# Differential attention's keys and queries: rounded on all 128 rows at once, then placed by transfers within SBUF

## The chip, the cores and the metric

The kernel runs on one core of a Trainium2 chip. The metric is the device time of one execution in microseconds (us), median of three runs. TensorE (PE) multiplies matrices, VectorE (DVE) and ScalarE (ACT) do elementwise work and empty PSUM, GpSimd (POOL) does small work, SyncE (SP) issues most of the transfers.

## What is computed

The reference is a two-layer transformer over 256 latent and 256 context tokens of width 1024. Each layer has a feed-forward part, a token mixer (retention in 4 heads beside differential attention in 8 heads) and a second feed-forward part. The change is in the differential attention, whose core is:

```python
q_d = rope_2d(to_diff_heads(dq), row, col)
k_d = rope_2d(to_diff_heads(dk), row, col)
k_all = jnp.concatenate([k_dc, k_d], axis=3)      # context keys are not rotated
s = jnp.einsum('bhiqd,bhikd->bhiqk', q, k) * (DIFF_DH ** -0.5)   # DIFF_DH = 64, two maps
p = jax.nn.softmax(s, axis=-1)
a = p[:, :, 0] - lam * p[:, :, 1]
o = jnp.einsum('bhqk,bhke->bhqe', a, v)
```

Each head has two maps of 64 channels. The rotation turns pairs of channels by an angle that depends on the token's row and column on the grid.

## The kernel before

Weights come from HBM in tiles of 128 x 1024 float32 (`load`, L143, four buffers `raw`, issued on SP). `split` (L151) makes of each a rounded part (ACT, L154) and the rest (DVE, L155) in a tile `w` (five buffers), and every product of a projection is made of three matmuls (`mm3`, L329 to L332): high x high, high x low, low x high. Activations `h` are kept in the same two parts.

The mixer (L451) walks through blocks of the input projection. `projT` (L521) computes a block with channels on the partitions (48 matmuls, of 512 columns for both token groups or 256 for the latents alone), into a pair of PSUM banks or one bank of the ring `main4`; `tok` (L497) computes a block with tokens on the partitions (24 matmuls into one bank). When a block is done, an eviction function empties the bank, and the bank goes back to the ring; the next block that gets it must wait for the eviction's last read.

`diff_blocks(u)` (L871) makes a unit: two heads, one K block (latent and context), then one Q block (both groups in layer 0, the latents in layer 1). There are four units in each of the two layers, and after each of them come token blocks (`rv_block` or `wide`). Its eviction is `ev_diff` (L564). For the latent columns it first calls `rotate` (L545): the block times the cosines (L547), products of row groups with the sines of the partner rows (L550, four groups of 32 rows for this table, two of 64 for the retention's), and a sum (L552). Then, for each of the two maps, it works on the 64 rows that belong to the map. For K, `KH[m]` must hold the rounded key in both halves of the 128 rows, `KL[m]` the rest in both halves: three copies on ACT (L575, L577, L578) and one subtraction on DVE (L576). For Q, `Q[m]` holds the rounded query in the map's own rows (ACT, L571) and the rest in the other rows (DVE, L572), so that one matmul with `KH[m]` (L660) and one with `KL[m]` (L661) give a map's score.

The scores, their softmax, the transposes and the products with V (`diff_attn`, L643) are side work: a generator in a queue, from which `tick` (L476) takes steps at given points of the projections, as many as are due; its argument is how much the point counts. `need` (L489) takes steps until a piece of side work is done. A planner in the framework then orders each engine's instructions and sets the waits on semaphores: the order on an engine is fixed before the run, but it is not simply the order of the source. SP works its queue in order, too: an issue that waits holds up the issues behind it.

`main4` is the ring of PSUM banks that projections use, `side4` that of the side work; `slot` gives one of 20 SBUF tiles of 4 KB per row (`r` in the trace), `tmp4` one of three of the same size (`t4`), which the scores' exponentials use, and `tmp2` one of five of 2 KB (`t2`).

Of the kernel before, what the change touches and what calls it, by code (L numbers as in the profile page):

```python
# [11 lines left out]
F32 = mybir.dt.float32  # L12
F32R = mybir.dt.float32r
BF16 = mybir.dt.bfloat16
AF = mybir.ActivationFunctionType
ALU = mybir.AluOpType
# [18 lines left out]
def build(ctx, tc, a):  # L35
# [415 lines left out]
    def mixer(l, st, AB, fetch, after):  # L451
# [69 lines left out]
        def projT(b, pairs, ev, w):  # L521
            ws = [split(r) for r in load(a["winT"][l, b])]
            n = 256 * len(pairs)
            if len(pairs) == 2:
                b0 = main4.two()
                bk = b0
            else:
                b0 = main4.one()
                bk = b0.rearrange("p (j n) -> p j n", j=2)
            for j in range(2):  # L530
                js = slice(j * P, (j + 1) * P)
                for k in range(KD):
                    wt = ws[k // 4].rearrange("p s (k n) -> p s k n", k=4)
                    mm3(bk[:, j], wt[:, 0, k % 4, js], wt[:, 1, k % 4, js], h[k // 2][:, k % 2, 0, 0:n],
                        h[k // 2][:, k % 2, 1, 0:n], k == 0, k == KD - 1)
                    if k == 7 and j == 0:
                        flush()
                    if j * KD + k in ((3, 7, 11) if len(pairs) == 2 else (7,)):
                        tick(w)
            for c in pairs:  # L540
                ev(c, bk[:, :, c * 256:(c + 1) * 256])
            main4.put(b0)
            tick(w)

        def rotate(b, tab, half):  # L545
            q, w = tmp2([P, 2, 256]), tmp2([P, 2, 256])
            dve.tensor_tensor(out=q, in0=b, in1=tab[:, 0].unsqueeze(1).broadcast_to([P, 2, 256]), op=ALU.mult)  # L547
            for p0 in range(0, P, half):
                p1 = p0 ^ half
                dve.tensor_tensor(out=w[p0:p0 + half], in0=b[p1:p1 + half],  # L550
                                  in1=tab[p0:p0 + half, 1].unsqueeze(1).broadcast_to([half, 2, 256]), op=ALU.mult)
            dve.tensor_tensor(out=q, in0=q, in1=w, op=ALU.add)  # L552
            return q
# [7 lines left out]
                                         op0=ALU.mult, op1=ALU.subtract)  # L561
            return ev

        def ev_diff(H, Lo):  # L564
            def ev(c, b):
                q = rotate(b, dtab, 32) if c == LAT else b
                sl = slice(c * 256, (c + 1) * 256)
                for m in range(2):
                    own, oth = slice(64 * m, 64 * m + 64), slice(64 - 64 * m, 128 - 64 * m)
                    if Lo is None:  # L570
                        act(H[m][own, :, sl], q[own], AF.Copy, scale=0.125)  # L571
                        dve.scalar_tensor_tensor(out=H[m][oth, :, sl], in0=q[own], scalar=0.125,  # L572
                                                 in1=H[m][own, :, sl], op0=ALU.mult, op1=ALU.subtract)
                    else:
                        nc.scalar.copy(H[m][own, :, sl], q[own])  # L575
                        dve.tensor_tensor(out=Lo[m][own, :, sl], in0=q[own], in1=H[m][own, :, sl], op=ALU.subtract)  # L576
                        nc.scalar.copy(H[m][oth, :, sl], q[own])  # L577
                        nc.scalar.copy(Lo[m][oth, :, sl], Lo[m][own, :, sl])  # L578
            return ev

        def ev_V(dst):
# [289 lines left out]
        def diff_blocks(u, before=None):  # L871
            KH = [slot([P, 2, 512], F32R) for _ in range(2)]
            KL = [slot([P, 2, 512], F32R) for _ in range(2)]
            projT(8 + u, BOTH, ev_diff(KH, KL), 0.3)
            if before:
                before()
            Q = [slot([P, 2, 512], F32R) for _ in range(2)]
            projT(4 + u, QP, ev_diff(Q, None), 0.3)
            return KH, KL, Q

        def diff_defer(u, kq, dv, within):
# [224 lines left out]
def rope_tables():  # L1106
    def ang(pos, half):
        inv = (np.float32(10000.0) ** (-np.arange(half, dtype=np.float32) / np.float32(half))).astype(np.float32)
        return (pos.astype(np.float32)[:, None] * inv[None, :]).astype(np.float32)

    t = np.arange(T)
    r = ang(t, 64)
    c, s = np.cos(r), np.sin(r)
    rt = np.stack([np.concatenate([c, c], 1), np.concatenate([-s, s], 1)], 0)
    d = np.concatenate([ang(t // 64, 16), ang(t % 64, 16)], 1)
    c, s = np.cos(d), np.sin(d)
    dt = np.stack([np.concatenate([c, c, c, c], 1), np.concatenate([-s, s, -s, s], 1)], 0)

    def lay(z):
        return np.ascontiguousarray(z.transpose(2, 0, 1), dtype=np.float32)  # L1120
    return lay(rt), lay(dt)
# [6 lines left out]
def layout(i):  # L1128
    f = {k: np.asarray(v) for k, v in i.items()}
    a = {}  # L1130
    a["xin"] = np.concatenate([f["x"][0], f["ctx"][0]], 0).reshape(4, P, D)
    a["ccc"] = np.stack([f["c"][0], f["c_ctx"]], 1).reshape(KD, P, 2).transpose(1, 0, 2)
    a["sel"] = (np.arange(P)[:, None] % 32 == np.arange(2)[None, :]).astype(np.float32)
    a["wada0"] = f["w_ada"][0, :, 0:2 * D].reshape(KD, P, 2, 4, 256).transpose(3, 1, 0, 2, 4).reshape(4, P, 4096)
    a["cc"] = np.stack([f["c"][0], f["c_ctx"]], 0)
    a["wada"] = f["w_ada"].transpose(0, 2, 1).reshape(L, 36, 2, P, D).transpose(0, 1, 3, 2, 4).reshape(L, 36, P, 2 * D)
    a["bada"] = f["b_ada"].reshape(L, 9, 8, P).transpose(3, 0, 1, 2)
    a["nwc"] = f["norm_w"].reshape(L, 6, 8, P).transpose(3, 0, 1, 2)
    a["fin"] = (f["ffn_w_in"].reshape(L, 2, KD, P, 2, NF, P).transpose(0, 1, 5, 3, 2, 4, 6)
                .reshape(L, 2, NF, P, 2048))  # L1140
    a["fout"] = f["ffn_w_out"].reshape(L, 2, NF // 2, 2, P, D).transpose(0, 1, 2, 4, 3, 5).reshape(L, 2, NF // 2, P, 2048)
    cols = np.arange(8192)
    cols[3072:5120] = cols[3072:5120].reshape(32, 2, 2, 16).transpose(0, 2, 1, 3).reshape(-1)
    wi = f["w_in"][:, :, cols].reshape(L, KD, P, 32, 256)
    a["winT"] = wi[:, :, :, TB].transpose(0, 3, 2, 1, 4).reshape(L, 12, P, 2048)
    a["winW"] = wi[:, :, :, WB].reshape(L, KD, P, 10, 512).transpose(0, 3, 2, 1, 4).reshape(L, 10, P, 4096)
    a["wout"] = f["w_out"].reshape(L, 4, 2, P, D).transpose(0, 1, 3, 2, 4).reshape(L, 4, P, 2048)
    a["gnw"] = f["ret_gn_w"]
    a["subw"] = f["diff_subln_w"]
    a["lamv"] = f["diff_lambda"]  # L1150
    a["decay"] = f["ret_decay_logit"].reshape(L, 8)
    a["rtab"], a["dtab"] = rope_tables()
    a["strip"] = strip_table()
    return {k: np.ascontiguousarray(v) for k, v in a.items()}
# [16 lines left out]
```

## Time and profile before

| | us |
|---|---|
| three runs, median | 2194.53 (2194.24 to 2195.38) |
| the profiled execution | 2194.1 |
| its span, first to last instruction | 2192.3 |
| PE busy | 2140.4 (98%) |
| DVE busy | 1365.7 (62%) |
| ACT busy | 865.8 (39%) |
| mean granted clock of TensorE | 0.996 |

Between the span and the execution lie 1.8 us. Busy time of PE counts a matmul to its modelled end, so that neighbours overlap: matmuls of 512 columns are 0.39 us long and start 0.227 us apart. The mixer of layer 0 lies between about 400 and 860 us of the span, that of layer 1 between about 1635 and 1990.

### The profile page before, as it was taken

How to read it: one execution, taken by the hardware profiler on the slowest of the kernel's cores; microseconds unless marked ns; L12 is line 12 of the kernel's file. 1: busy time of each engine (PE TensorE's matmuls, PEld its weight loads, DVE VectorE, ACT ScalarE, POOL GpSimd, SP SyncE). 2: the span in 40 equal slices, each digit the busy share in tenths (PEclk: the TensorE clock that was granted, in tenths of full speed). 3: DMA queues.
4: the chain of work that ended last, by engine and by line, in shares of the span. 5: the costliest groups of instructions: out<-in, count | busy, mean ns of one | idle time of the engine just before them, and what ended most of it. 6: DMA issues, size and time to landing. Idle time of an engine off the chain costs nothing. (4 is left out here: it accounts for less than half of the span.)

```text
span 2192.3 us, 27590 instructions
## 1 busy us (share of the span) xinstructions
PE 2140.4 (98%) x10730; PEld 1790.6 (82%) x10730; DVE 1365.7 (62%) x2108; ACT 865.8 (39%) x1367; POOL 129.1 (6%) x236
## 2 busy tenths in 40 slices
PE   7999999999999999999999999999999999998998
PEld 5888888778788878888888888888878888878997
DVE  4799372678665774596243279825347776787554
ACT  3322332553533553522232242223245544565453
POOL 1000000201010000200000010000010000001000
PEclk9999999999999999999999999999999999999999
DMA  8866342222122234364334247734323323355554
GB/s 332 284 218 217 106 135 96 88 68 85 51 91 98 68 97 148 132 211 155 97 124 139 91 161 224 269 96 134 97 67 109 115 93 108 123 194 174 187 183 134
DMA packets 85060, 306.99 MB, mean 140 GB/s; under 512 B 9968, under 2 KB 10048, under 8 KB 84928
## 3 DMA queue, kind: packets, MB, share of 16 engines
q1 hardware_dynamic: 81936, 296.78, 41.2%
q0 software_dynamic: 2848, 8.43, 1.4%
q8 instruction: 84, 1.38, 0.3%
q14 instruction: 48, 0.39, 0.1%
q10 hardware_dynamic: 144, 0.01, 0.0%
HBM read 304.10 MB, written 1.09 MB: 139 GB/s over the span
## 5 line engine op out<-in xcount | busy, mean ns | idle before, releaser
L155 DVE TENSOR_TENSOR w<-raw,w 128x1024 fp32r<-128x1024 f32 x408 | 497.2, 1222 | 465.6 <-ACT w L154 461.9
L154 ACT CAST w<-raw 128x1024 fp32r<-128x1024 f32 x408 | 427.5, 1053 | 665.4 <-PE ps L332 609.3
L330 PE MATMUL ps<-h,w 128*128 128x512 f32 (+1 forms) x1868 | 664.7, 357 | 4.7 <-ACT w L154 2.6
L331 PE MATMUL ps<-h,w 128*128 128x512 f32 (+1 forms) x1868 | 664.9, 356 | 0.4 <-DVE h L293 0.3
L332 PE MATMUL ps<-h,w 128*128 128x512 f32 (+1 forms) x1868 | 663.6, 356 | 1.2 <-DVE w L155 1.2
L330 PEld LDWEIGHTS ps<-h,w 128*128 128x128 f32 x1868 | 353.4, 190 | 57.2 <-DVE h L292 4.7
L332 PEld LDWEIGHTS ps<-h,w 128*128 128x128 f32 x1868 | 353.8, 190 | 50.6 <-DVE w L155 1.8
L331 PEld LDWEIGHTS ps<-h,w 128*128 128x128 f32 x1868 | 354.1, 190 | 50.2 <-DVE h L293 1.4
L174 DVE CUSTOM_DVE_ANT_0 jd<-r,r 128x1024 bf16<-128x1024 f32 x224 | 273.4, 1221 | 6.8 <-DMA r<-wada_dram 2.0
L330 PE MATMUL ps<-w,h 128*128 128x512 f32 x544 | 216.1, 398 | 15.5 <-ACT r L577 11.9
L331 PE MATMUL ps<-w,h 128*128 128x512 f32 x544 | 214.3, 394 | 0.0
L332 PE MATMUL ps<-w,h 128*128 128x512 f32 x544 | 213.8, 394 | 0.0
L330 PE MATMUL ps<-w,gs 128*128 128x512 f32 x504 | 196.2, 389 | 0.0
L331 PE MATMUL ps<-w,gs 128*128 128x512 f32 x504 | 196.1, 389 | 0.0
L332 PE MATMUL ps<-w,gs 128*128 128x512 f32 x504 | 196.1, 389 | 0.0
L366 ACT ACTIVATE t<-ps 128x512 f32<-128x512 f32 (+1 forms) x88 | 47.9, 545 | 252.0 <-PE ps L332 250.6
L330 PEld LDWEIGHTS ps<-w,h 128*128 128x128 f32 x544 | 102.7, 189 | 38.2 <-ACT r L577 15.2
L367 DVE TENSOR_TENSOR r<-ps,t 128x512 f32<-128x512 f32 (+1 forms) x88 | 54.8, 622 | 105.3 <-PE ps L332 77.7
L331 PEld LDWEIGHTS ps<-w,h 128*128 128x128 f32 x544 | 102.8, 189 | 20.2 <-DVE w L155 1.5
L332 PEld LDWEIGHTS ps<-w,h 128*128 128x128 f32 x544 | 102.5, 188 | 20.4
L330 PEld LDWEIGHTS ps<-w,gs 128*128 128x128 f32 x504 | 94.6, 188 | 19.8
L332 PEld LDWEIGHTS ps<-w,gs 128*128 128x128 f32 x504 | 94.6, 188 | 19.6
(180 smaller groups left out, 2132.8 us busy)
## 6 DMA issues: line engine op xcount, KB each, us to landing
raw<-fin_dram SPq DMA_DIRECT2D x176, 512.0 KB, 4.3
r<-wada_dram SPq DMA_DIRECT2D x144, 512.0 KB, 5.1
raw<-fout_dram SPq DMA_DIRECT2D x88, 512.0 KB, 3.6
raw<-winW_dram SPq DMA_DIRECT2D x80, 512.0 KB, 3.6
raw<-winT_dram SPq DMA_DIRECT2D x48, 512.0 KB, 3.6
raw<-wout_dram SPq DMA_DIRECT2D x16, 512.0 KB, 5.6
r<-scr POOLq DMA_DIRECT2D x10, 512.0 KB, 5.4
r<-cc_dram SPq DMA_DIRECT2D x7, 512.0 KB, 5.2
```

The costliest lines, as they stand in the source:

```text
L154: keep(nc.scalar.copy(w[:, 0, :], src))
L155: keep(dve.tensor_tensor(out=w[:, 1, :], in0=src, in1=w[:, 0, :], op=ALU.subtract))
L174: dve.tensor_tensor_reduce(out=junk, in0=r[j], in1=cs[c], scale=1.0, scalar=0.0, op0=ALU.mult, op1=ALU.add, accum_out=out[:, c, 2 * u + j: ...
L330: mm(o, lhsT=wH, rhs=xH, start=start, stop=False)
L331: mm(o, lhsT=wH, rhs=xL, start=False, stop=False)
L332: mm(o, lhsT=wL, rhs=xH, start=False, stop=stop)
L366: act(sg[:, :N], ab[0][:, :N], AF.Silu)
L367: dve.tensor_tensor(out=g[f // 2][:, f % 2, :N], in0=ab[1][:, :N], in1=sg[:, :N], op=ALU.mult)
```

## The change

The four parts belong together.

1. `ev_diff` becomes `ev_full`, which is like the eviction of the retention's projections: one copy or scaling on ACT for all 128 rows and one subtraction on DVE.
2. The halves that the maps' tiles need are made by transfers: `move` copies two groups of 32 rows (rows 32m to 32m+31 and 64+32m to 64+32m+31) from one SBUF tile to the same or the other groups of another, in two DMAs on SP. A unit has 12 of these for K and 8 for Q. Q's parts are first put into two `t4` tiles. The third move of each K tile writes rows that the first two have read.
3. The columns of the input projection are put in another order (on the host), so that the two halves of a rotation lie 64 rows apart, and the signs in the sine table follow. `rotate` then runs two products of 64 rows instead of four of 32.
4. `projT` evicts the context columns before the latent ones (for the retention's projections, too), and the differential projections count 0.5 per tick point instead of 0.3.

```diff
-            for c in pairs:
+            for c in reversed(pairs):
                 ev(c, bk[:, :, c * 256:(c + 1) * 256])
...
-        def ev_diff(H, Lo):
+        def rows_of(m):
+            return [slice(32 * m + 64 * x, 32 * m + 64 * x + 32) for x in range(2)]
+
+        def move(dst, md, src, ms, n):
+            for rd, rs in zip(rows_of(md), rows_of(ms)):
+                nc.sync.dma_start(dst[rd, :, 0:n].bitcast(F32), src[rs, :, 0:n].bitcast(F32))
+
+        def ev_full(H, Lo, scale):
             def ev(c, b):
-                q = rotate(b, dtab, 32) if c == LAT else b
+                q = rotate(b, dtab, 64) if c == LAT else b
                 sl = slice(c * 256, (c + 1) * 256)
-                for m in range(2):
-                    own, oth = slice(64 * m, 64 * m + 64), slice(64 - 64 * m, 128 - 64 * m)
-                    if Lo is None:
-                        act(H[m][own, :, sl], q[own], AF.Copy, scale=0.125)
-                        dve.scalar_tensor_tensor(out=H[m][oth, :, sl], in0=q[own], scalar=0.125,
-                                                 in1=H[m][own, :, sl], op0=ALU.mult, op1=ALU.subtract)
-                    else:
-                        nc.scalar.copy(H[m][own, :, sl], q[own])
-                        dve.tensor_tensor(out=Lo[m][own, :, sl], in0=q[own], in1=H[m][own, :, sl], op=ALU.subtract)
-                        nc.scalar.copy(H[m][oth, :, sl], q[own])
-                        nc.scalar.copy(Lo[m][oth, :, sl], Lo[m][own, :, sl])
+                act(H[:, :, sl], q, AF.Copy, scale=scale)
+                dve.scalar_tensor_tensor(out=Lo[:, :, sl], in0=q, scalar=scale, in1=H[:, :, sl],
+                                         op0=ALU.mult, op1=ALU.subtract)
             return ev
...
-            projT(8 + u, BOTH, ev_diff(KH, KL), 0.3)
+            projT(8 + u, BOTH, ev_full(KH[0], KL[0], 1.0), 0.5)
+            for K2 in (KH, KL):
+                move(K2[1], 1, K2[0], 1, 512)
+                move(K2[1], 0, K2[0], 1, 512)
+                move(K2[0], 1, K2[0], 0, 512)
             if before:
                 before()
             Q = [slot([P, 2, 512], F32R) for _ in range(2)]
-            projT(4 + u, QP, ev_diff(Q, None), 0.3)
+            qH, qL = tmp4([P, 2, 512], F32R), tmp4([P, 2, 512], F32R)
+            projT(4 + u, QP, ev_full(qH, qL, 0.125), 0.5)
+            for m in range(2):
+                move(Q[m], m, qH, m, 256 * NQ)
+                move(Q[m], 1 - m, qL, m, 256 * NQ)
             return KH, KL, Q
...
-    dt = np.stack([np.concatenate([c, c, c, c], 1), np.concatenate([-s, s, -s, s], 1)], 0)
+    dt = np.stack([np.concatenate([c, c, c, c], 1), np.concatenate([-s, -s, s, s], 1)], 0)
...
-    cols[3072:5120] = cols[3072:5120].reshape(32, 2, 2, 16).transpose(0, 2, 1, 3).reshape(-1)
+    cols[3072:5120] = cols[3072:5120].reshape(16, 2, 2, 2, 16).transpose(0, 3, 1, 2, 4).reshape(-1)
```

## Rows read from the trace of the kernel before

**Rows 1.** The page, first part: busy us (share of the span) x instructions.
```profile
PE 2140.4 (98%) x10730; PEld 1790.6 (82%) x10730; DVE 1365.7 (62%) x2108; ACT 865.8 (39%) x1367; POOL 129.1 (6%) x236
```
**Rows 2.** Waits of PE, 390 to 870: total us, times, longest us.
```profile
PE ps L330 <- ACT r L577: 6.6, 4, 1.7
...
PE ps L660 <- DVE r L572: 0.3, 1, 0.3
```
**Rows 3.** Waits of PE, 1630 to 2000.
```profile
PE ps L330 <- ACT r L577: 5.3, 4, 1.4
PE ps L330 <- DVE t L550: 3.2, 1, 3.2
```
**Rows 4.** Timeline of PE, unit 0, layer 0: start, us, instruction [idle before <-releaser].
```profile
446.43 0.39 PE L331 MATMUL ps<-h,w 128*128 128x512 f32 x1
446.65 0.39 PE L332 MATMUL ps<-h,w 128*128 128x512 f32 x1
448.70 0.50 PE L330 MATMUL ps<-w,h 128*128 128x512 f32 x1 [1.66 <-ACT r L577]
```
**Rows 5.** Timeline of ACT in the same place: K's eviction.
```profile
442.24 0.62 ACT L577 CAST r<-t 64x512 fp32r<-64x512 f32 x1
...
448.07 0.58 ACT L577 CAST r<-ps 64x512 fp32r<-64x512 f32 x1
```
**Rows 6.** Timeline of DVE in the same place.
```profile
436.20 0.69 DVE L547 TENSOR_TENSOR t<-ps,dtab 128x512 f32<-128x512 f32 x1 [0.41 <-PE ps L332]
436.90 2.79 DVE L550 TENSOR_TENSOR t<-ps,dtab 32x512 f32<-32x512 f32 x4
439.72 1.22 DVE L155 TENSOR_TENSOR w<-raw,w 128x1024 fp32r<-128x1024 f32 x1
...
442.24 0.68 DVE L576 TENSOR_TENSOR r<-t,r 64x512 fp32r<-64x512 f32 x1
```
**Rows 7.** DVE's groups by line and shape, whole span: xcount | busy us, mean ns.
```profile
L550 DVE TENSOR_TENSOR t<-ps,rtab 64x512 f32<-64x512 f32 x16 | 11.0, 688 | 0.2
```
**Rows 8.** Timeline of PE, last unit of layer 1.
```profile
1919.07 0.39 PE L330 MATMUL ps<-w,h 128*128 128x512 f32 x1
1922.67 0.47 PE L330 MATMUL ps<-w,h 128*128 128x512 f32 x1 [3.21 <-DVE t L550]
1924.09 0.50 PE L330 MATMUL ps<-w,h 128*128 128x512 f32 x1 [0.95 <-ACT r L577]
```
**Rows 9.** Two stretches: length, busy us of PE, PEld, DVE, ACT, POOL, PEclk, DMA share, GB/s.
```profile
446.00:450.00 4.00, 2.34 (x11) 1.62 (x10) 2.47 (x3) 3.92 (x6) 0.00 (x0) 1.00 0.00 0
1923.00:1929.00 6.00, 5.05 (x15) 3.87 (x15) 5.82 (x7) 3.72 (x6) 0.00 (x0) 0.72 0.28 87
```
**Rows 10.** The page, DMA issues: xcount, KB each, median us from issue to landing.
```profile
raw<-winT_dram SPq DMA_DIRECT2D x48, 512.0 KB, 3.6
...
gnb<-gnw_dram POOLq DMA_DIRECT2D x8, 128.0 KB, 3.2
out_dram<-X SPq DMA_DIRECT2D x4, 256.0 KB, 2.1
```
**Rows 11.** Timeline of SP and ACT after unit 0; SP's issues of `raw` (ns).
```profile
429.65 20.12 SPq L147 DMA_DIRECT2D raw<-winT_dram  x4
...
479.17 2.18 ACT L154 CAST w<-raw 128x1024 fp32r<-128x1024 f32 x2
...
L147 SPq DMA_DIRECT2D raw<-winT_dram x3: 327/328/328, 435.8 to 449.4; - x3
```
**Rows 12.** Timeline of DVE and PE, first score of unit 0.
```profile
456.27 1.40 DVE L572 SCALAR_TENSOR_TENSOR r<-t,r 64x512 fp32r<-64x512 f32 x2
...
457.01 0.50 PE L660 MATMUL ps<-r,r 128*128 128x512 f32 x1
```
**Rows 13.** SP in the first 30 us: timeline, and its waits in the whole span.
```profile
9.52 10.82 SPq L999 DMA_DIRECT2D r<-wada_dram  x8
...
SPq L999 <- DMA r<-wada_dram: 6.5, 7, 0.9
```

## Prediction: what the change does to the time

> **What bounds the kernel now.** I began with the page's first part: TensorE (PE) is busy 98% of the span, VectorE (DVE) 62%, ScalarE (ACT) 39% [rows 1]. So only what PE loses can be won; less work on DVE or ACT is worth nothing by itself. Next came the waits of PE alone, in the stretches of the two mixers. In layer 0 one wait stands out: the first product of a product series waits four times for line 577, 6.6 us together, and nothing else that the change touches reaches 0.4 us [rows 2]. In layer 1 the same wait takes 5.3 us in four places, and a wait for line 550 takes 3.2 us once [rows 3]. Lines 550 and 577 are both evictions of a differential projection. There are 8 units (four in each of two layers), and each has one such place.
>
> The timeline shows one place. The Q projection's last product starts at 446.65; the next token product starts at 448.70, released by ACT line 577 [rows 4]. Products start 0.22 us apart otherwise, so 1.82 us are lost. The token product needs a PSUM bank of the *K* projection, which had ended before DVE began its rotation at 436.20 [rows 6]. From there to the last read of that bank, at 448.07 + 0.58 = 448.65 [rows 5], go 12.4 us. The reader sees why: DVE takes four 32-row products (2.79 us together) before ACT can start [rows 6], then ACT makes 12 half-width copies of about 0.6 us, with a weight cast between them. Each copy covers 64 partitions but costs what 512 columns cost.
>
> **The change, part by part.** The time of an instruction here goes by its columns: the 32-row products take 0.70 us each [rows 6], the 64-row products of the retention table 0.688 us [rows 7]. So two products of 64 rows replace four of 32 at the same price each, and one full-width copy replaces six half ones.
>
> K's eviction becomes: context first, one ACT copy (0.6) and one DVE subtraction (0.69), then for the latent columns one product, two products and a sum (four of 0.69) and again one copy and one subtraction. The bank's last PSUM read is the second 64-row product: 436.20 + 0.6 + 0.69 + 3 x 0.69 = 439.6, or 440.8 with the weight subtraction of 1.22 us that DVE had in between [rows 6]. PE asks for the bank at 446.65 + 0.23 = 446.9. A margin of 6 us remains, so this wait goes entirely. In layer 1 the Q product series has half as many columns, but there PE passes through one whole token tile before it asks.
>
> What goes: layer 0, 4 x 1.82 = 7.3 us. Layer 1, first three places: idle 5.3 - 0.95 = 4.35 [rows 3, 8], plus 0.17 each, since idle counts from a product's end (0.39 long) and not from the next start at 0.22: 4.85 us. The last place is the worst: starts at 1919.07, 1922.67 and 1924.09 [rows 8] lose 3.37 + 1.19 us as shown, but a row of line 330 follows another of line 330 twice, so products of lines 331 and 332 are missing from the trace; with two missing at each gap 3.65 is left, with more about 3.0. I take 3.4. After it the granted clock is 0.72 over 6 us, a mean of full (2.4 GHz) and half (1.2 GHz), where it was 1.00 around the wait of the first unit [rows 9]: 6 x 0.28 = 1.7 us more. Sum: 7.3 + 4.85 + 3.4 + 1.7 = 17.2 us.
>
> What comes: per unit 12 moves of K and 8 of Q, 32 rows each, 128 KB (Q in layer 1: 64 KB), all on SP's queue. No row shows a transfer from SBUF to SBUF. The nearest rows: a 128 KB load lands in 3.2 us, a 256 KB store in 2.1, a 512 KB load in 3.6 [rows 10]; I take 2.1 to 3.6, and 2.7 as the middle. Issue takes 0.33 us each [rows 11]: 20 issues are 6.6 us of SP per unit.
>
> Queued behind the moves on SP are the weight loads. Four loads issued from 429.65 to 449.77 [rows 11] feed splits of which the next but one starts at 479.17 [rows 11], since `raw` has four buffers; the last of the four lands about 453.4, 25 us early. The third K move of each tile must wait until the first two have been read (one landing), so K blocks SP for about 0.33 x 6 + 2.7 = 5 us per tile, and Q's eight for about 5. That fits in 25 us; cost 0 in layer 0. Without that cover each us is a us of PE. Writes to other rows of one tile don't wait for each other: ACT line 577 and DVE line 576 run in the same 442.24 to 442.86 on different halves [rows 5, 6].
>
> Who waits for the moves: the first score (line 660) of the unit. Today it starts at 457.01 [rows 12], right behind the last DVE work it needs (456.27, two of 0.70, the first done at 456.96) [rows 12], and 36 products of 0.227 us have run since 448.70: the planner orders PE by when operands are ready, with token products ahead as filler. New chain: Q ends at 447.0, ACT 0.6, DVE 0.69 + 2.76 + a weight subtraction 1.22, ACT 0.62, DVE 0.69 gives 453.0 at most; the four moves of map 0 are issued by 453.7 and land by 455.8 to 457.3. PE, 1.8 us earlier, has then run 40 to 46 of the four token tiles' 96 products. So Q arrives about when it does now, since the work that DVE and ACT save pays for the moves. What it costs depends on where the planner puts the score, which no row shows: between 0 and 2.1 us a unit (order unchanged, 36 products from 446.9 end at 455.2, against 457.3). I take 0.3, because today's order meets its operands within 0.3 us [rows 2]: 8 x 0.3 = 2.4 us.
>
> The tick weight of 0.5 for 0.3 moves side steps forward and adds no work; today the wait for a side step's operands is 0.3 us where it is longest among the units' scores [rows 2], so 0, within 8 x 0.3 = 2.4 us either way. Two `t4` buffers for Q's halves are taken while no score runs (the side work is drained by then in units 1 to 3): 0. The reversed order of columns in the retention projections swaps two evictions of one bank, which is free only after both: 0.
>
> Forecast: the profiled execution took 2194.1 us (span 2192.3), 0.4 below the median of the runs. 2194.1 - 17.2 + 2.4 = **2179 us**.
>
> **A rule against the change.** Startup shows SP limited by landings: eight loads of 512 KB are issued over 10.82 us, 1.5 us apart, and SP waited seven times for an earlier transfer [rows 13]. The Trainium skill, "DMA: Bandwidth & Descriptors", Rules for kernel authors, says of two transfers to disjoint partition halves "Don't bother — they serialize", and asks for one 128-partition transfer; here each move is such a pair. By that rule the moves queue, which is the slower rival below, priced there from rows; no run here shows it yet. [...]
>
> **Rivals.**
> *Order misses the landing.* The score stands where it does today, 0.6 to 2.1 us too early. 8 x 1.35 = 11 us come back: 2194.1 - 17.2 + 11 = 2188. For it: PE's order is fixed before the run, and planning of such transfers is untested in this trace. Against: the exact fit of today's order.
> *Moves queue (slower).* If the transfers follow each other at the 1.5 us of rows 13 instead of 0.33, map 0's four moves land 4 x 1.17 = 4.7 us later in every unit, and K's chain pushes in front. At line 660 PE loses 4.7 x 8 = 37 us, against 17.2 won: 2214; if each such pause also lowers the clock as after 1924, 8 x 1.7 more: 2228. It decides from 2.1 us per unit upward. Against: 512 KB were moved there, here a quarter.
> *The bank is not it.* Another wait follows at once, for instance the token product's fourth weight tile, and the time stays at 2190 to 2198. Against: with ACT's copies gone, that weight cast comes earlier, too.
>
> **How the numbers follow.** Forecast (2174 to 2184) 0.60; order misses the landing (2184 to 2192) 0.17; nothing won (2190 to 2198) 0.09; moves queue (2199 to 2228) 0.11; more won than counted, because freed DVE and ACT also shorten small waits, 0.03. What this kernel's measurement can tell from no change is about 0.2%, 4.4 us, so faster means below 2190.1. Range 2174 to 2194: it holds the forecast, the second case and half of the third. Faster: 0.60 + 0.03 + 0.13 = 0.76; same: 0.12; slower: 0.12.
>
> **What would show it.** In the waits of PE the rows for line 577 are gone and no row for the new eviction exceeds 0.3 us; the clock stays at 1.00 in the last unit. In the issues, 128 KB moves land in 2.1 to 3.6 us. SP's waits grow, without a wait of ACT for a `raw` load. Wrong would be: PE waiting for a DMA at line 660 by more than 2 us a unit, or for weights.

## The result: slower by 1.0%, and the profile after

The changed kernel takes 2217.4 us (median; 2214.4 to 2218.4) beside 2194.4 us of the kernel before on the same chip: a ratio of 1.0103, 95% interval 1.0085 to 1.0120. The forecast was 2179 us, faster by 0.7%, with a range of 2174 to 2194. It was wrong in sign.

The profiled execution has a span of 2215.0 us. The page's first part, beside [rows 1]:

```profile
PE 2148.0 (97%) x10730; PEld 1802.5 (81%) x10730; DVE 1317.6 (59%) x2048; ACT 807.4 (36%) x1275; POOL 131.0 (6%) x236
```

DVE and ACT lost the work that the change takes away (48 and 58 us), PE has the same 10730 products, and the span grew all the same. The reader looks for the place next. Each mixer and each feed-forward stage begins with transpositions at line 280 behind a norm, so the starts of these cut the trace into stages. The first one of mixer 0, its end, and the same for mixer 1: 390.80, 893.25, 1629.55, 1993.63 before; 392.89, 910.08, 1644.72, 2016.13 after. So mixer 0 grew from 502.5 to 517.2 us and mixer 1 from 364.1 to 371.4; what lies between them takes 736.3 and 734.6. The 2.1 us ahead of mixer 0 are no part of the change: over all profiled runs below, whose startup is the same, that mark lies between 390.4 and 393.3.

The wait that the prediction aimed at is gone. Timeline of PE in unit 0, where [rows 4] had a pause of 1.66 us:

```profile
448.75 0.39 PE L332 MATMUL ps<-h,w 128*128 128x512 f32 x1
448.98 0.39 PE L330 MATMUL ps<-w,h 128*128 128x512 f32 x1
```

The query's last product is followed by the first token product at the usual distance. But the waits of PE in mixer 0 (393 to 911; total us, times, longest) are now these, where [rows 2] had one line of weight:

```profile
PE ps L330 <- DVE t L550: 6.0, 2, 3.0
PE ps L659 <- ACT t L664: 3.8, 2, 3.0
...
PE ps L860 <- ACT t L664: 2.3, 1, 2.3
PE ps L693 <- ACT t L683: 2.0, 4, 0.5
PE ps L681 <- DVE es L698: 1.6, 2, 0.8
```

and in mixer 1 (1645 to 2017), against [rows 3]:

```profile
PE ps L331 <- DVE w L155: 3.3, 2, 2.9
PE ps L332 <- DVE w L155: 2.9, 1, 2.9
PE ps L330 <- DVE t L842: 2.0, 1, 2.0
```

No row names a DMA: PE never waits for a transfer. It waits for the differential units' own softmax chain (lines 664 to 698: exponentials, transposed copies, turns and weighings), for line 550, now the rotation of the *retention* query, and for weight splits. The page's list of DMA issues has the transfers themselves (count, KB, median us to landing), and the timeline of SP shows their first block:

```profile
r<-r SPq DMA_DIRECT2D x96, 128.0 KB, 2.3
...
444.17 7.19 SPq L569 DMA_DIRECT2D r<-r  x10
455.05 0.51 SPq L569 DMA_DIRECT2D r<-t  x1
455.65 1.17 SPq L569 DMA_DIRECT2D r<-r  x2
456.88 4.39 SPq L569 DMA_DIRECT2D r<-t  x7
461.31 0.58 SPq L147 DMA_DIRECT2D raw<-winT_dram  x1
```

Landing is as quick as predicted. The last of unit 0's twenty transfers goes out at 460.7 and ends its issue at 461.3; with 2.3 us to landing all have landed by some 463. Now the scores of unit 0, from the timeline of PE: the first score's map 0, its map 1, the third score, the last one, the turn behind it, the last weighing and the next token product (a turn is the transposition of a block of softmax weights on PE, line 681; a weighing is the product of such a block with V, line 693).

```profile
471.64 0.39 PE L659 MATMUL ps<-r,r 128*128 128x512 f32 x1
...
477.99 0.39 PE L659 MATMUL ps<-r,r 128*128 128x512 f32 x1
...
482.52 0.39 PE L659 MATMUL ps<-r,r 128*128 128x512 f32 x1
...
501.76 0.37 PE L659 MATMUL ps<-r,r 128*128 128x256 f32 x1
...
506.47 0.41 PE L681 MATMUL ps<-ident,t 128*128 128x128 f32 x2 [0.77 <-DVE es L698]
508.79 0.71 PE L693 MATMUL ps<-r,t 128*128 128x128 f32 x4 [0.52 <-ACT t L683]
512.47 0.79 PE L330 MATMUL ps<-w,h 128*128 128x512 f32 x1 [2.97 <-DVE t L550]
```

The first score starts without any wait at 471.64, some 8 us after its tiles were complete, and 22.7 us after the token products began (8.3 us in [rows 4, 12]). It stands in PE's fixed program behind all 96 token products of the block. The first two scores are laid together, and their halves of map 1 stand 24 products behind those of map 0; the third score stands 16 behind that. So the products that could have covered the softmax chain have been spent early, and from 506 on PE runs dry. On DVE (timeline) one sees whom the next token product waits for:

```profile
508.26 1.23 DVE L155 TENSOR_TENSOR w<-raw,w 128x1024 fp32r<-128x1024 f32 x1 [0.35 <-ACT w L154]
509.40 0.68 DVE L547 TENSOR_TENSOR t<-ps,rtab 128x512 f32<-128x512 f32 x1
510.22 0.69 DVE L703 TENSOR_REDUCE oss<-t 128x4 f32<-128x512 f32 x1
510.94 0.69 DVE L550 TENSOR_TENSOR t<-ps,rtab 64x512 f32<-64x512 f32 x1
511.56 0.15 DVE L705 SCALAR_TENSOR_TENSOR ms<-oss,es 128x4 f32<-128x4 f32 x1
511.73 0.68 DVE L550 TENSOR_TENSOR t<-ps,rtab 64x512 f32<-64x512 f32 x1
```

The rotation of a retention projection, whose bank PE needs, stands between a weight split and the unit's own normalisation. A bank wait went from one projection to another. The clock falls too. In two stretches (columns as in [rows 9]) the granted clock is 1.00 ahead of the pauses and 0.62 with them and behind them, a mean of full and half (2.4 and 1.2 GHz), 9 x 0.38 = 3.4 us:

```profile
500.00:506.00 6.00, 5.70 (x33) 4.44 (x31) 4.84 (x13) 3.81 (x12) 1.04 (x1) 1.00 0.00 0
509.00:518.00 9.00, 6.03 (x18) 4.66 (x18) 8.33 (x17) 2.02 (x4) 1.56 (x2) 0.62 0.25 84
```

With its waits (0.77 + 2 x 0.5 + 2.97 = 4.7 us) the tail of unit 0 costs about 8 us. Unit 1 repeats this, units 2 and 3 vary it. Over both mixers there are five such stretches (510 to 518, 633 to 641, 749 to 753, 1930 to 1941 and 1967 to 1972, at 0.57, 0.57, 0.57, 0.53 and 0.66), some 15 us together.

### The profile page after: what moved, and what is told of

The parts are those of the page before. It is cut to its first block, busy times and chain, and to the rows that moved or that the text cites. A ratio compares the mean times of both kernels' runs of the same rounds, so it can differ in the third digit from the quotient of the medians.

```text
span 2215.0 us, 27737 instructions
## 1 busy us (share of the span) xinstructions
PE 2148.0 (97%) x10730; PEld 1802.5 (81%) x10730; DVE 1317.6 (59%) x2048; ACT 807.4 (36%) x1275; POOL 131.0 (6%) x236
```

## Experiments

The question was where the 17 us won and some 23 more went. The theories, as the expectations name them: A, the first score stands later; B, the transfers hold up the weight loads behind them on SP; C, pacing, reversal or the two more buffers; D, how the side work of a unit meets other work and filler; E, the number of transfers in a row. Each kernel was timed against the kernel before on the same chip. All results first, so that the stages can be compared (us; mixers between the marks at line 280 of the profiled execution):

| kernel | median | ratio to before, 95% interval | mixer 0 | mixer 1 | first score, unit 0 |
|---|---|---|---|---|---|
| before | 2194.4 | | 502.5 | 364.1 | 457.0 |
| changed | 2217.4 | 1.0103 (1.0085 to 1.0120) | 517.2 | 371.4 | 471.6 |
| no_moves | 2174.1 | 0.9907 (0.9893 to 0.9922) | 493.4 | 353.7 | 454.3 |
| late_scores | 2195.0 | 1.0004 (0.9995 to 1.0014) | 501.7 | 365.7 | 475.7 |
| act_moves | 2193.9 | 0.9996 (0.9986 to 1.0005) | 495.6 | 370.2 | 466.6 |
| pool_moves | 2208.9 | 1.0061 (1.0044 to 1.0078) | 504.3 | 379.7 | 471.1 |
| no_rev | 2211.1 | 1.0076 (1.0061 to 1.0091) | 517.0 | 368.8 | 469.9 |
| mv64_sp | 2181.5 | 0.9942 (0.9925 to 0.9958) | 493.5 | 360.3 | 461.3 |
| eng_copies | 2181.4 | 0.9942 (0.9928 to 0.9957) | 495.9 | 358.4 | 459.4 |
| early_bank | 2183.1 | 0.9949 (0.9935 to 0.9964) | 498.6 | 357.1 | 458.9 |
| pin72 | 2191.3 | 0.9983 (0.9974 to 0.9992) | 498.3 | 364.4 | 462.8 |
| pin48 | 2218.0 | 1.0107 (1.0090 to 1.0124) | 505.9 | 386.4 | 460.5 |
| later_scores | 2208.7 | 1.0065 (1.0050 to 1.0080) | 510.6 | 370.5 | 487.2 |
| mvK_engQ | 2177.6 | 0.9923 (0.9909 to 0.9938) | 494.1 | 355.5 | 457.5 |

### Without the transfers

```diff
-            for K2 in (KH, KL):
-                move(K2[1], 1, K2[0], 1, 512)
-                move(K2[1], 0, K2[0], 1, 512)
-                move(K2[0], 1, K2[0], 0, 512)
-            qH, qL = tmp4([P, 2, 512], F32R), tmp4([P, 2, 512], F32R)
-            projT(4 + u, QP, ev_full(qH, qL, 0.125), 0.5)
-            for m in range(2):
-                move(Q[m], m, qH, m, 256 * NQ)
-                move(Q[m], 1 - m, qL, m, 256 * NQ)
+            projT(4 + u, QP, ev_full(Q[0], Q[1], 0.125), 0.5)
```
and the scores read KH[0] and KL[0] for both maps.

> The changed kernel without its transfers: keys and queries are evicted on all 128 rows as there, then nothing is placed. Left out is the placement alone: both maps' scores read the same two key tiles, and the tiles of Q hold the rounded query and its rest, so the scores are other numbers, with the same instructions on the engines, the same pacing (0.5) and the same reversal. Theory A (the first score stands later in TensorE's order, because the tiles come late through the transfers; the side work is then bunched and runs out of filler): without transfers the scores stand early again, no wait for a key or query eviction is left, and the 17 us of the prediction's first step appear: 2175 to 2182 us. Theory B (the 20 transfers hold up the weight loads behind them on SP's queue): they are gone too, the same 2175 to 2182. Theory C (the pacing, the reversal or the two more tiles of the ring of three cost the time): it stays above 2205.

Measured: 2174.1 us. So the first step of the prediction holds, and was even too small: 20.6 us go (2194.7 to 2174.1), where it had 17.2. The first score stands at 454.3, and no wait of PE in mixer 0 beyond the norm's exceeds 0.6 us:

```profile
PE ps L693 <- DVE r L712: 0.6, 1, 0.6
PE ps L681 <- DVE t L672: 0.5, 2, 0.2
```

Theory C falls as far as pacing and reversal alone go: both are in this kernel. (Its third part, the two `t4` tiles, goes here together with the transfers; a kernel below that keeps the tiles, mvK_engQ, takes 2177.6 us, so there they cost little.) What the transfers bring costs 2217.4 - 2174.1 = 43 us, 23.8 in mixer 0 and 17.7 in mixer 1.

### Late scores without transfers

```diff
-        diff_defer(0, kq, dv, pick(11, 10))
         rv_block(0)
+        diff_defer(0, kq, dv, pick(3, 2))
```
and the same for unit 1.

> The kernel before, with one thing changed: the scores of heads' units 0 and 1 are put on the side queue after the block of four token products instead of ahead of it, with the deadline kept (within 3 and 2 instead of 11, 10 and 9). Nothing is evicted or moved otherwise, and no transfer is added; units 2 and 3 stay. In each of four units the first score then stands 95 to 96 token products and 12 products of the next projection behind the query, instead of 35 to 48. Theory A: each of these units pays for the bunched side work what it pays in the changed kernel; there the four units of layer 0 lost about 14.7 + 8 = 23 us, some 5.7 us a unit, and layer 1 some 7.3 + 6 = 13 us, so four units of the eight give 14 to 20 us: 2206 to 2216 us. Theory B (SP's queue): nothing is on SP that was not there, 2192 to 2197 us.

Measured: 2195.0 us, no difference. Theory A in the form "a late first score costs time" falls: here it starts at 475.67, later than in the changed kernel. The timeline of PE (the first score's map 0 and map 1, the third score, the last one, the turn) tells why lateness alone is harmless:

```profile
475.67 0.39 PE L660 MATMUL ps<-r,r 128*128 128x512 f32 x1
...
476.12 0.39 PE L660 MATMUL ps<-r,r 128*128 128x512 f32 x1
...
480.20 0.50 PE L660 MATMUL ps<-r,r 128*128 128x512 f32 x1
...
500.14 0.28 PE L660 MATMUL ps<-r,r 128*128 128x256 f32 x1
...
507.45 0.39 PE L682 MATMUL ps<-ident,t 128*128 128x128 f32 x2
```

Map 1 follows map 0 at once (476.12), the third score comes 4.5 us after the first and not 10.9, and the products saved there, 28 in place of 12, stand between the last score's weighing and the turn at 507.45, which has no wait. So it is not where the scores begin but how the products around them are spent that makes the difference. In the changed kernel the halves of a score are laid 24 products apart, as if the second map's transfers were taken to arrive later. That is an argument from the order; what the planner assumes of a transfer, no trace shows.

### Another queue

act_moves:
```diff
-                nc.sync.dma_start(dst[rd, :, 0:n].bitcast(F32), src[rs, :, 0:n].bitcast(F32))
+                nc.scalar.dma_start(dst[rd, :, 0:n].bitcast(F32), src[rs, :, 0:n].bitcast(F32))
```
and pool_moves has `pool.dma_start` in the same place.

> The changed kernel with its 20 transfers a unit issued on ScalarE's queue instead of SP's. The plan then puts the first score of layer 0's units behind 73 token products instead of 96 and 4 of the next projection; layer 1's unchanged or nearly so. SP's queue holds weight loads alone. Theory A: the place of the score rules, and 23 of the about 65 products of delay against the kernel before are given back: layer 0 gains some 23/65 of 23 us = 8 us and layer 1 little, 2202 to 2211 us, less what issuing costs ScalarE. Theory B: SP's queue is free, the late weights are gone, 2177 to 2185 us.

> The changed kernel with its transfers issued on GpSimd's queue instead of SP's. The plan puts the first scores where the changed kernel has them (behind all 96 token products and 3 of the next projection in layer 0, 12 in layer 1), but nothing stands ahead of the weight loads on SP's queue. Theory A: layer 0 loses what it loses in the changed kernel, 2207 to 2217 us, with the waits for late weights (3.06 us at 1918 and at 1967 us, and what the halved clock behind them costs) gone at most: 6 to 10 us. Theory B: 2177 to 2187 us.

Measured: 2193.9 and 2208.9 us. Neither theory has the first number; the second lies in A's range. SP holds weight loads alone in both, and 20 and 35 us of the 43 are still there, so B is not the whole cause; but each of these queues brings a cost of its own, so they don't tell B's share. With ACT's queue mixer 0 is nearly free of cost (495.6 against 493.4): its first score stands at 466.6. Mixer 1 loses 16.5 us, and there at last PE waits for landings. Waits of PE in mixer 1 of act_moves, then the timeline of ACT ahead of the first of them:

```profile
PE ps L659 <- DMA r<-t: 12.5, 2, 7.2
```
```profile
1866.51 12.20 ACTq L569 DMA_DIRECT2D r<-r  x10
1878.76 0.63 ACT L575 ACTIVATE t<-t 128x512 fp32r<-128x512 f32 x1 [11.32 <-DMA r<-r]
```

Ten moves hold ACT for 12.2 us, half of it for their issue, half because the third move of each key tile overwrites rows that two others read and waits for their landing; the query's rounding stands behind it. In the stretch 1862 to 1888 a move takes 2.0 to 7.9 us to land, median 2.3, as weight loads run on SP at the same time. On GpSimd's queue the moves land in 3.9 us (median), and mixer 1 is the longest but one of all, with 4.3 us of PE's waits for DMA and 6.3 us for the softmax chain.

Mixer 0 of pool_moves shows that the place of the first score is not all either. The score stands where the changed kernel has it (471.1), its halves are 24 products apart, too, and yet mixer 0 pays 10.9 us over no_moves and not 23.8. The bank wait is nearly gone (waits of PE in mixer 0, 6.0 us above):

```profile
PE ps L330 <- DVE t L550: 1.3, 2, 0.7
```

In the changed kernel two weight splits stand on DVE in the tail of unit 0, at 504.71 and 508.26; in pool_moves there is none between 500 and 513. The weight loads go out earlier there, from 453.4 instead of 461.9. So some 13 us of mixer 0's cost go when the moves leave SP's queue, though no engine waits for a weight load in this mixer in either kernel; whether the later loads themselves or only the planned order put the splits into the tail, no run separates.

### The order of the two evictions put back

```diff
-            for c in reversed(pairs):
+            for c in pairs:
```

> The changed kernel with the order of the two evictions of a projection put back (latents first, then context, as in the kernel before); transfers, layout and pacing as changed. In TensorE's order the first score of units 0 and 1 stands only 6 products earlier than in the changed kernel, still behind 94 token products, but between the last two weighings of a unit there now stand 3 and 10 products of other work, where the changed kernel has none. Theory D (what costs layer 0 its time is that the last turns and weighings of a unit, and the bank that the retention query's rotation frees, follow one another without filler: 0.93 + 0.62 + 0.68 + 3.14 us and 3.4 us of halved clock, twice): units 0 and 1 lose some 2 us instead of 8.8, 13 us less: 2201 to 2208 us. Theory B (only SP's queue): 2214 to 2222. Rival to both, the reversal itself freed the banks: above 2220.

Measured: 2211.1 us, 6 less than the changed kernel and above the range of theory D. Mixer 0 did not change (517.0). The last turns and weighings of units 0 and 1 have filler now and wait less; but the wait for the retention projection's bank is a little longer than the 6.0 us of the changed kernel, as PE's waits in mixer 0 show:

```profile
PE ps L330 <- DVE r L560: 6.8, 2, 3.4
```

So of theory D the missing filler is the lesser part, and the bank is what stays: with the context's columns evicted last it is freed by the rounding at line 560 on DVE, again late.

### Half as many transfers

The layout of the kernel before (halves 32 rows apart, a map's rows together), one move of 64 rows for two of 32:

```diff
+            for K2 in (KH, KL):
+                move_sp(K2[1][R[1]], K2[0][R[1]])
+                move_sp(K2[1][R[0]], K2[0][R[1]])
+                move_sp(K2[0][R[1]], K2[0][R[0]])
...
+                move_sp(Q[m][R[m], :, n], qH[R[m], :, n])
+                move_sp(Q[m][R[1 - m], :, n], qL[R[m], :, n])
```

> The changed kernel with the layout of the kernel before (rotation halves 32 rows apart, so that a map's rows lie together) and one transfer of 64 rows where the changed kernel has two of 32: 10 a unit instead of 20, on SP as there; pacing 0.3. The first scores stand behind 56 token products (64 in layer 1) instead of 100. Theory E (the number of transfers in a row on the queue decides, through their issue and through the place of the scores): half of the cost of the transfers, which is 2217 - 2174 = 43 us, or less: 2183 to 2196 us. If instead the landing of one transfer decides, and not their number: 2205 to 2217 us.

Measured: 2181.5 us, under the range of theory E and 36 us below the changed kernel. Mixer 0 is where it is without transfers (493.5). The first score stands at 461.3, without a wait. The bytes are the same, and each transfer lands later. The list of issues has the median over the whole span, then the first move of a block, with no other move in flight, and the last move of unit 0's query (issued at 457.9):

```profile
r<-r SPq DMA_DIRECT2D x48, 256.0 KB, 4.5
...
r<-r SPq DMA_DIRECT2D x1, 256.0 KB, 3.0
...
r<-t SPq DMA_DIRECT2D x1, 256.0 KB, 5.0
```

So the median is in good part that of moves piling up: the query's last tile is complete at 457.9 + 5.0 = 462.9, where the changed kernel has it at 460.7 + 2.3 = 463.0. Bytes and landing are the same, and the first score stands 10.4 us earlier. So neither sets the cost; it goes with the number of transfers, by way of the order. (The layout and the pacing of this kernel are those of before, too. no_moves has the changed ones and loses nothing by them without transfers; with transfers they were not tried apart.) What is left is in mixer 1, five waits for weight splits (longest 2.7 us, total in the waits of PE there):

```profile
PE ps L331 <- DVE w L155: 4.8, 5, 2.7
```

### Placement by copies, and an earlier bank

eng_copies: the same rounding on all rows, the ten moves made by ACT and DVE (`nc.scalar.copy`, `dve.tensor_copy`). early_bank: the kernel before with two edits,

```diff
-            for c in pairs:
+            for c in reversed(pairs):
...
-                        nc.scalar.copy(H[m][oth, :, sl], q[own])
-                        nc.scalar.copy(Lo[m][oth, :, sl], Lo[m][own, :, sl])
+                if Lo is not None:
+                    for m in range(2):
+                        own, oth = slice(64 * m, 64 * m + 64), slice(64 - 64 * m, 128 - 64 * m)
+                        nc.scalar.copy(H[m][oth, :, sl], H[m][own, :, sl])
+                        nc.scalar.copy(Lo[m][oth, :, sl], Lo[m][own, :, sl])
```

> No transfers: keys and queries are evicted on all 128 rows at once as in the changed kernel, in the layout of the kernel before (rotation halves 32 rows apart), and placed in the maps' tiles by ten copies of 64 rows in SBUF, four to seven on ScalarE and the rest on VectorE. Full computation. Theory A, B and D alike (the transfers, through the queue, the landing or the place of the scores, cost all of the 43 us): the scores stand behind 44 to 47 products, the bank is free after the rounding, and the time is that without placement plus what the copies delay: 2174 to 2184 us. If the copies on ScalarE and VectorE put back the wait that the kernel before has: 2188 to 2196 us.

> The kernel before with two small edits: the context's columns are evicted ahead of the latents' (the reversal of the change), and the second copy of a key's rounded half reads the first copy in SBUF instead of the bank, after both maps' roundings. Nothing moves by transfer, and no row is evicted more or less often. If the bank is what TensorE waits for at the query, two of the four copies of the context's keys no longer hold it, some 2 x 0.6 us earlier of the 1.8 us waited, and the rest goes with the reversal: 2178 to 2188 us. If it is the amount of eviction work, whatever its order: 2192 to 2197 us.

Measured: 2181.4 and 2183.1 us, both as expected. A few lines that only reorder who reads the bank when win 11 us: the bank was the thing to free, and the two ways of doing the work on the engines differ by 1.7 us only.

### An earlier place for the scores, transfers kept

```diff
+        def behind_score():
+            return tc.issue_after(firsts[since[0]]) if since[1] > 3 and since[0] in firsts else nullcontext()
+
+        def tok(ws, t, ev):
+            since[1] += 1
+            with behind_score():
+                tok_in(ws, t, ev)
...
+        def projT(*z):
+            with behind_score():
+                projT_in(*z)
```
`since` holds the unit last put on the side queue and the token blocks since then, `firsts` the last product of each unit's first score; pin48 has 2 in place of 3.

> The changed kernel, transfers and all, with one edge of order added per unit: what TensorE's program has from the fourth token block after the query on is queued behind the unit's first score. The first score then stands behind 72 token products instead of 96 and 4 of the next projection. In the changed kernel the transfers of unit 0's query have landed at 463.0 us, and 72 products after the query end at 465.4: no wait for them in layer 0. Theory D (the place of the scores: they stand 8 us later than their tiles allow, and the side work then meets the retention query's rotation on VectorE): layer 0 takes 493 to 498 us instead of 517, layer 1 keeps its late weights: 2189 to 2199 us. If the transfers cost as such, by queue or by landing, wherever the scores stand: 2209 to 2219 us.

> As the one before, with the edge one token block earlier: the first score stands behind 48 products after the query, at some 460 us for unit 0, while the last of the transfers of its query lands at 463.0. So this is the case that the prediction named as the rival in which TensorE meets transfers in flight: a wait of some 3 us for a tile that a transfer writes in each unit of layer 0 and at least as much in layer 1, and the halved clock after some of them. 6 to 8 units of 3 to 5 us above the kernel with the edge at 72: 2205 to 2230 us. If the place is again all that counts, and landing nothing: 2185 to 2195 us.

Measured: 2191.3 and 2218.0 us. With nothing but edges of order added, the changed kernel gets 26 us faster, and mixer 0 takes 498.3 us (in the profiled execution, which is with 2187.7 us the fastest of ten). In pin72 the first score's map 0 and map 1 are together again (timeline of PE), no bank wait is left in mixer 0, and the longest wait that is left there is this:

```profile
462.80 0.39 PE L673 MATMUL ps<-r,r 128*128 128x512 f32 x1
...
463.70 0.39 PE L673 MATMUL ps<-r,r 128*128 128x512 f32 x1
```
```profile
PE ps L673 <- ACT t L679: 3.0, 3, 1.1
```

One token block earlier all of it is lost again, and now it is the landing, with the half clock behind such pauses. PE's timeline in pin48, and its waits in mixer 1:

```profile
463.12 0.47 PE L673 MATMUL ps<-r,r 128*128 128x512 f32 x1 [1.42 <-DMA r<-t]
```
```profile
PE ps L673 <- DMA r<-t: 13.6, 6, 6.1
```

The 463.12 is the arrival of the last tile of map 1, told by the engine that waited for it. So a place 2.6 us ahead of the landing (460.5) costs as much as one 8 us behind it, by a different mechanism. What pin72 still has over no_moves lies mostly in mixer 1 (10.7 us), among it one wait of 2.9 us for a weight split.

### Still later scores without transfers

As late_scores, with the unit put on the side queue between the two projections of `rkq_blocks`.

> The kernel before, without transfers, with units 0 and 1 put on the side queue still later than in the run with late scores: between the two projections of the retention block, with the deadline within 3 and 2. The first score stands behind 95 token products and 60 of the next projections, 11 us later than there, and the plan leaves products between all turns and weighings. Theory D (lateness costs only where it brings the side work onto the eviction that frees the next block's bank): here the retention query's rotation falls into the middle of the side work, so units 0 and 1 of both layers pay 3 to 6 us each: 2204 to 2218 us. If lateness without transfers costs nothing at any place: 2193 to 2198 us.

Measured: 2208.7 us, in the range; but the waits are only in part those of theory D. One 4.3 us wait comes from a retention head's own side step, which had been pushed back with the rest, and 6.7 us are bank waits at line 550 in mixer 1, 3.2 of them as before [rows 3]. So lateness costs nothing at 475.7 and 14 us at 487.2. What it meets there decides.

### Keys by transfer, query by copies

```diff
             for K2 in (KH, KL): move_sp(...)   # six moves of 64 rows
...
+                nc.scalar.copy(Q[m][R[m], :, n], qH[R[m], :, n])
+                dve.tensor_copy(Q[m][R[1 - m], :, n], qL[R[m], :, n])
```

> Rounding on all rows at once, layout of the kernel before; the keys are placed by six transfers of 64 rows on SP, the query by four copies of 64 rows in SBUF on ScalarE and VectorE. Full computation. The keys' transfers have the query's projection (some 11 us in layer 0, 6 in layer 1) to land in, the query needs none, and SP holds six transfers in a row instead of ten or twenty. Theory E (number of transfers in a row on the queue): below the kernel with ten transfers and with ten copies: 2175 to 2181 us, with a wait for landing in layer 1 as what is left. If the two only add what each costs: 2180 to 2186 us.

Measured: 2177.6 us, a ratio of 0.9923 to the kernel before (0.9909 to 0.9938): the fastest kernel here that does the whole computation. The keys' transfers have a whole projection to land in; the query has none to wait for. The wait for landing that was expected in layer 1 did not come; what is left there is 1.6 us in four waits for weight splits.

## Why the prediction was wrong, point by point

**The bank, 17.2 us: right.** All eight waits went, and the kernel without transfers is 20.6 us faster than before: 9.1 in mixer 0 (7.3 said) and 10.4 in mixer 1 (9.95 with the clock, of which below).

**Landing, 2.7 us: right**, 2.3 us at the median. **Chain to the query: right.** The first move of the query was forecast for 453.0 with PE at 446.9; it went out at 455.05 with PE at 449.0, the same distance.

**Issue, 0.33 us each, and cost 0 on SP in layer 0: too small, and the cost is not shown to be 0.** A move of 32 rows holds SP for 0.58 us at the median. Unit 0's block on SP takes 17.1 us (444.17 to 461.31) with its waits, where the prediction had about 5 us for each key tile and 5 for the query, 15 in all. In layer 0 the cover of 25 us took it as far as waits for a load go: no engine waits for one there. But taking the moves off SP gave back some 13 us of mixer 0 (pool_moves), which the prediction's account of SP has no term for. For layer 1 the prediction said that each us without cover is a us of PE and put no number to it. ACT's waits for `raw` loads, which its signs excluded, grow there from 1.0 to 7.5 us. PE waits for weight splits, too, which it named as a sign of being wrong, but at the two longest waits the weight had been cast in time and only the split was late. One of them (timelines of ACT, DVE and PE):

```profile
1912.35 1.04 ACT L154 CAST w<-raw 128x1024 fp32r<-128x1024 f32 x1
...
1914.68 2.35 DVE L661 TENSOR_REDUCE mx<-ps 128x2 f32<-128x1024 f32 x2 [1.50 <-PE ps L660]
1916.95 1.21 DVE L155 TENSOR_TENSOR w<-raw,w 128x1024 fp32r<-128x1024 f32 x1
...
1918.22 0.39 PE L332 MATMUL ps<-h,w 128*128 128x256 f32 x1 [2.89 <-DVE w L155]
```

The cast is done at 1913.4 and DVE sits idle until 1914.7, but two reductions of scores stand ahead of the split in DVE's program; at the other (1966.9) it is the same, with the cast done at 1962.4. Order again; what the loads behind the moves had to do with that order in layer 1 was not tried apart from the rest.

**The place of the score, 0.3 us a unit: this is the step that failed.** The prediction wrote that the cost "depends on where the planner puts the score, which no row shows", and then took 0.3, "because today's order meets its operands within 0.3 us". That row shows that the order fitted the engines' work. It says nothing of an order with twenty transfers in a row, of which this trace had none. The bounds of 0 and 2.1 us a unit were both worked out for a score that is too *early*. That an order can miss on the other side, too late and with its halves apart, was in neither bound nor in any rival. The first score came at 471.6, 22.7 us behind the start of the token products, where the prediction had 8 to 10; the term of 2.4 us for all eight units stands against 43 us measured for all that the transfers bring. It costs by collisions and not by a wait at the score: PE's waits in the mixers, the norm's left out, add up to 18.9 and 13.9 us where no_moves has 1.6 and 1.0, and the five stretches at half clock cost some 15 us where no_moves has 1.7; the two overlap and cover the 41.5 us of both mixers. Moving the scores takes 26 of the 43 us off (pin72). Of the other 17 about 5 are in mixer 0, where waits for exponentials are left (line 679, 5.2 us), and 11 in mixer 1, with waits for a weight split (2.9), for other side work (2.0), for the softmax chain (2.7) and for landings (1.1) and a stretch at half clock. Why the order has these is open; without the transfers they are gone.

**The rivals.** "Order misses the landing" is a real case, but as pin48, which had to be built. "Moves queue" gave 2214 to 2228, and the time fell into it, but its mechanism is not in the changed kernel: no wait for a DMA in the mixers. **The rule against the change.** Two moves of a pair go out 0.6 us apart and each lands in 2.3 us, so the pair is down some 2.9 us after its start; one move of the same bytes on 64 rows, with none in flight, lands in 3.0 us (mv64_sp). The Trainium skill, "DMA: Bandwidth & Descriptors", Rules for kernel authors, says of two transfers to disjoint partition halves that they serialize, and asks for one 128-partition transfer. In landing the pair and the single move are alike here, so these rows neither bear the rule out nor speak against it, and no run has a move of 128 rows. Moves queueing on landings, the rival that was drawn from it, did not come: but for the third move of each key tile they go out every 0.6 us. For the kernel's time one transfer in place of two was better by 36 us, by the place of the scores.

**The clock, 1.7 us: right where it was read, but no gain in the sum.** The half clock at 1924 is gone without transfers, but no_moves has one at 1622 to 1626 (0.57 over 4 us, 1.7 us) that the kernel before has not, and its mean clock is 0.994 against 0.996. That the first step came out at 17.2 or more all the same is luck as far as this term goes. In the changed kernel the mean is 0.989.

**Reversal and pacing, 0: right as far as tried.** no_moves has both and takes 2174.1 us; with the transfers, putting the reversal back gains 6 us (0.2 in mixer 0, 2.6 in mixer 1 of the profiled execution). The pacing was not tried alone with the transfers.

## What to carry to other kernels

Where a planner fixes the order of each engine, a new kind of operation changes the order before it costs any time itself: look at where the consumers stand in the new program, and bound a misplacement on both sides, too early (a wait for data) and too late (fillers spent, other work met). Freeing the resource that is waited for can often be had by reordering reads of it (11 us for a few lines here), without a new path for the data. And put transfers where a whole stage lies ahead of the consumer, few and wide, as the keys here, and keep the short path for what is needed at once, as the query: that was the fastest whole kernel here.

## What the hardware showed that was not expected

A transfer within SBUF of 32 rows holds the queue's engine for 0.58 us where a load of 128 rows from HBM holds it for 0.33 [rows 11]. 128 KB on 32 rows land in 2.3 us, with three or four such moves in flight 0.6 us apart. 256 KB on 64 rows land in 3.0 us alone; put out some 0.6 us apart they pile up, to 5.0 us for the fourth, so that the query of unit 0 is complete at the same time with either (463.0 and 462.9). On ScalarE's queue beside weight loads on SP the same moves took up to 7.9 us and held ScalarE's own work for 11.3 us, by their issue and by the wait of one move for another. And pauses of a few us in PE came with a stretch at half clock, so that the tail of unit 0 cost about 8 us where its waits add up to 4.7.
